# Splitting the gate of a Mamba-2 mixer group in two, and moving its state-space part behind a column tile

## The chip, the cores and the metric

The kernel runs on one core of one Trainium2 chip. The metric is the device time of one execution in microseconds (us); the median of a few runs is given with the lowest and the highest. The engines are called as the profile calls them: PE (matrix products) with its weight loads PEld, DVE (VectorE), ACT (ScalarE), POOL (GpSimd) and SP (SyncE, which issues the DMAs).

## The reference, cut to what matters

The program is one step of a decoder layer for 256 prompt tokens and 8 sample tokens (264 columns): a half-step feed-forward block, a token mixer, a second half-step feed-forward block and a per-layer embedding. The change is in the mixer. One projection gives 81 column tiles of 128 features, and 8 state-space groups share them: a group has one tile each of B and C, three of x and three of z. Cut to the state-space part:

```python
proj = u @ w_in                       # -> glu_a, glu_b, z, xbc, dt_raw
v = glu_a * sigmoid(glu_b)            # 8 tiles; causal convolution of width 31, LayerNorm, swish
xbc = silu(causal_dwconv(xbc, ...))   # width 4 -> xs, B, C
dt = softplus(dt_raw + dt_bias)
y, h_new = ssd(xs, dt, a, B, C, d_skip, h0)   # chunked scan, chunks of 128 tokens
yg = y * silu(z)                      # the gate
yg = yg * rsqrt(mean(yg * yg over the group's 384 features) + EPS) * ssm_norm_g
out = concat([v, yg]) @ w_out
```

## The kernel before, in words

Features lie on partitions and tokens on columns. A column tile of a projection is 48 products on PE: 16 row tiles times 3, because weights and activations are split into two float32r halves (lines 244 to 246). The weights are streamed: a load on SP's queue (L150, two of 512 KB a column tile), a rounding on ACT (`whi`, L151), the remainder on DVE (`wlo`, L152). A result goes to one of five `acc` banks in PSUM; three further banks (`ps`) serve all the smaller products.

The loop over `IN_ORDER` goes through the projection's tiles: first dt, then for each group g the tiles B, C, x0, x1, x2, z0, z1, z2, and in groups 1, 2, 4 and 6 a pair of GLU tiles (gb, ga) behind x0; the last four GLU pairs (4 to 7) follow group 7. What happens to a finished tile:

- B, C, x: `do_conv`, a short convolution (ACT, then DVE) and a SiLU on ACT. The three x tiles of a group share a buffer `xt`, its three z tiles a buffer `zs`. `xt`, `zs` and the result `y` come from one tag, `h`, with four buffers (the trace calls all of them h).
- `decays(g)`, behind x0: loads of cumulated decays, and Exps on ACT.
- `ssd(g, ...)`, the state-space part, behind x2: transposes on PE (L688, L689), products (L702, L714, L729, L736), the first write of `y` (a DVE operation on the products of L729), then the sample tokens: two transposes (L742, L743), a copy, a store to DRAM and a broadcast load (`d_bc`, `cbc`), three loads of saved state with a product on POOL and a sum on DVE each, and a few small DVE operations, the last of which completes `y`.
- `gate(g, y, zs)`: a DVE product y * zs, three squares on ACT, two adds on POOL (`run`), the sum over partitions on PE (`total`, L296), Ln and Exp on ACT, and the scaled results on DVE. It is put into `pend` at z2 and run by `finish_gate` at the next group's x0, behind that tile's convolution and ahead of `decays`. That of group 7 runs behind GLU tile pair 4, and then the mixer's buffers are given up.
- GLU: three Exp/Ln operations on ACT and a product; the 30 steps of its convolution are put into a queue of filler operations (`bg`), of which the loop takes up to four behind each column tile.

What sets the order: the framework lists each engine's instructions when the program is built. It keeps an estimate of the time, and among the instructions whose inputs and buffers are ready by it, the one earlier in the program goes first; weight loads are marked to go ahead. The engines then run through these lists in order and wait for each other by semaphores. One order is written out by hand: functions on ACT that need a table (SiLU, Sigmoid, Exp, Ln) run in program order (`table`, `after`), so that the table changes only where the program changes from one kind to the other.

Of the kernel before, what the change touches and what calls it, by code (L numbers as in the profile page):

```python
# [41 lines left out]
# ---------------------------------------------------------------- layout plan  # L42
def _in_order():
    """Column tiles of the input projection in the order they are computed."""
    out = [("dt", MT_DT)]
    glu = 0

    def pair():
        nonlocal glu
        out.append(("gb", MT_B + glu))  # L50
        out.append(("ga", MT_A + glu))
        glu += 1

    for g in range(GRP):
        out.append(("B", MT_BM + g))
        out.append(("C", MT_CM + g))
        out.append(("x", MT_X + 3 * g))
        if g in GLU_IN:
            pair()
        out.extend(("x", MT_X + 3 * g + j) for j in (1, 2))  # L60
        out.extend(("z", MT_Z + 3 * g + j) for j in range(3))
    while glu < CM:
        pair()
    return out
# [5 lines left out]
def _plan():  # L70
    """Weight units in order of use: (matrix, row tiles, column tiles), row tile slowest."""
# [39 lines left out]
# columns of the small-parameter block  # L111
# [13 lines left out]
class Weights:  # L125
    """Streams the weight units: load, round to float32r, keep what rounding left."""
# [8 lines left out]
    def load(self, between=()):  # L135
        """The next unit, in halves; runs a function of `between` ahead of each half."""
# [29 lines left out]
def kernel(ctx: ExitStack, tc: tile.TileContext, a: dict):  # L166
# [10 lines left out]
    # ------------------------------------------------------------ helpers  # L177
# [50 lines left out]
    def table(name):  # L228
        """Functions that need a table run in program order, so that tables change only here."""
        if order["set"] != name:  # L230
            order["set"] = name
            after(nc.scalar.preload_act_table_set(name).ins)
# [15 lines left out]
    def split(x, gain=None):  # L248
        """float32r halves of x (times a gain per partition)."""
        t = act_tile()  # L250
        if gain is None:
            nc.scalar.copy(t[:, 0, :], x)  # L252
            tt(t[:, 1, :], x, t[:, 0, :].bitcast(F32), ALU.subtract)
        else:
            act(t[:, 0, :], x, AF.Identity, scale=gain)
            stt(t[:, 1, :], x, gain, t[:, 0, :].bitcast(F32), ALU.mult, ALU.subtract)
        return t

    class SumSq:
        """Sum of squares over tiles and partitions, on every partition. The last `direct` tiles  # L260
        go to the tensor engine by themselves."""
# [19 lines left out]
        def add_plain(self, s):  # L281
            """Adds the tile s itself."""
# [16 lines left out]
    def rsqrt(out, x, bias=0.0, scale=1.0):  # L299
        """(scale * x + bias) ** -0.5"""  # L300
        act(out, x, AF.Ln, bias=bias, scale=scale)
        act(out, out, AF.Exp, scale=-0.5)

    def rms_scale(p, n):
        """1 / sqrt(p / n + eps)"""
        r = rtile()
        rsqrt(r, p, eps1, 1.0 / n)
        return r

    # ------------------------------------------------------------ constants  # L310
# [10 lines left out]
    # ------------------------------------------------------------ residual stream  # L321
# [5 lines left out]
    bg = deque()  # work that fills in between the matrix products  # L327

    # ------------------------------------------------------------ feed-forward
# [22 lines left out]
    def ffn(xs, sq, done):  # L352
        """xs: split gained input; sq: its sum of squares. Calls done(m, y) on each finished
        column tile y (without the input scale); returns eps * (mean square + eps) of the input."""
# [42 lines left out]
    def ffn_scale(p, eq):  # L397
        """1 / 2 / sqrt(mean(y^2) + eps / scale^2): the post-norm of scale * y, halved, where
        eq = eps / scale^2."""
# [13 lines left out]
    # ============================================================ FFN 1  # L413
# [15 lines left out]
    # sample conv history: sums over the saved rows  # L429
# [33 lines left out]
    # y for the post-norm; h . y and y . y (with the gain) for the next pre-norm  # L463
# [22 lines left out]
    # mean square of h + rs y, from the parts  # L486
# [8 lines left out]
    # per-layer embedding projection: independent of the residual stream  # L495
# [13 lines left out]
    # u = rmsnorm(h + rs y), two tiles behind the update of h  # L509
# [15 lines left out]
    # ============================================================ mixer  # L525
# [3 lines left out]
    # causal triangle: row token s, column token l, l >= s  # L529
# [6 lines left out]
    tm = mp.tile([P, 2, 2, NH], F32, name="tm")          # token-major dt, dt*A per chunk  # L536
    acs = mp.tile([P, 2, NH], F32, name="acs")           # token-major cumulative sums
    dte = mp.tile([P, 2, NH], F32, name="dte")           # decay to the end of the chunk
    cd = mp.tile([P, NH], F32, name="cd")                # decay over chunk 1
    dtp = mp.tile([P, 24, NS], F32, name="dtp")          # sample dt on (head, p)  # L540
    eap = cpool.tile([P, 24, NS], F32, name="eap")       # sample decay on (head, p)
    xds = cpool.tile([P, 24, NS], F32, name="xds")       # sample x * dt on (head, p)
# [55 lines left out]
    def do_conv(acc, i, out):  # L598
        """Short causal convolution and SiLU of xBC tile i."""
# [9 lines left out]
    def keep(k, x):  # L609
        """A finished input tile of the output projection."""  # L610
# [46 lines left out]
    def decays(g):  # L657
        """Decay between the tokens of each chunk, and from the start of chunk 1."""
# [19 lines left out]
    def ssd(g, bf, cf, xt, ab, ea):  # L678
        """State-space part of group g: y before the gate, [128, 3, T]."""
        hs = slice(HPG * g, HPG * g + HPG)  # L680
        y = h_tile()[:, :3, :]
        # token-major x * dt and B
# [20 lines left out]
        # decay times C.B; the decay's exponent is never positive where l >= s  # L703
# [4 lines left out]
        # state after each chunk  # L708
# [15 lines left out]
        # outputs  # L724
# [14 lines left out]
        # sample tokens  # L739
# [29 lines left out]
    def gate(g, y, zs):  # L769
        tt(y, y, zs, ALU.mult)  # L770
        sq = SumSq(3, direct=0)
        for j in range(3):
            sq.add(y[:, j, :])
        t = tmp()
# [6 lines left out]

    def finish_gate():
        if pend:
            gate(*pend.pop())

    first = gemm_first(us, k16, 4)
    pend = []
    nglu = 0
    for n, (kind, m) in enumerate(IN_ORDER):
# [6 lines left out]
        elif kind == "C":  # L796
            do_conv(acc, m - MT_X, bct[:, 1, :])
        elif kind == "x":
# [7 lines left out]
            if j == 2:  # L806
                y = ssd(g, bct[:, 0, :], bct[:, 1, :], xt, ab, ea)
        elif kind == "z":
# [3 lines left out]
            act(zs[:, j, :], acc, AF.Silu)  # L812
            if j == 2:
                pend.append((g, y, zs))
        elif kind == "gb":
            pb = acc
        elif kind == "ga":
            do_glu(nglu, pb, acc)
            nglu += 1
            if nglu == len(GLU_IN) + 1:  # L820
                finish_gate()
# [9 lines left out]
    # output projection: the state-space rows, then the convolution rows  # L831
# [50 lines left out]
    # ============================================================ FFN 2  # L882
# [3 lines left out]
    def update(j, bb):  # L886
        """Sample state of head pair j: decay and add x dt (outer) B."""
# [37 lines left out]
    # ============================================================ per-layer embedding  # L925
# [32 lines left out]
# tiles (first, count) that each engine brings up to date in the last update  # L958
# [4 lines left out]
# ---------------------------------------------------------------- launch  # L963
# [16 lines left out]
def _feat(v):  # L980
    """(F, ...) -> [128, F/128, ...], feature = tile * 128 + partition."""
# [103 lines left out]
```

## Time and profile before

| | |
|---|---|
| runs | median 2482.04 us of 3 (2472.21 to 2486.53) |
| profiled execution, from its first to its last instruction | 2479.2 us |
| PE busy | 2405.7 us, 97% |
| DVE busy | 1593.6 us, 64% |
| ACT busy | 1179.2 us, 48% |
| POOL busy | 348.6 us, 14% |
| mean granted PE clock | 0.990 |
| DMA | 489.88 MB, mean 198 GB/s |

The profile gives no other time of its own execution than this span; it is 0.1% under the median of the runs. Busy times overlap, and PE's products are pipelined: a row gives a product some 0.28 us, though the next one starts 0.12 us later. "Idle before" or a bracket behind a row is the time that the engine stood still, with the instruction that ended it. The granted clock is the share of PE's full clock that the throttle let through.

### The profile page before, as it was taken

The page shows a single profiled execution, that of the slowest core. Times are in us where ns is not written, and L with a number is a line of the kernel's source. Part 1 is how long each engine was busy: PE and PEld are TensorE (multiplying, and loading weights), DVE is VectorE, ACT ScalarE, POOL GpSimd, SP SyncE. Part 2 cuts the span into 40 slices and gives each one's busy share as a digit, 9 for nine tenths or more (in the row PEclk, how much of TensorE's full clock was granted, in tenths as well). Part 3 has the DMA queues.
Part 4 walks back from the last instruction along what each step waited for, and adds up shares of the span by engine and source line. Part 5 has one row for each costly group of instructions (what it writes and reads, how often), then busy time and mean ns, then how long its engine had stood idle before and what let it go on. Part 6 is the DMA issues. An engine that isn't in the chain of part 4 may idle for free.

```text
span 2479.2 us, 47214 instructions
## 1 busy us (share of the span) xinstructions
PE 2405.7 (97%) x19432; PEld 2380.9 (96%) x19432; DVE 1593.6 (64%) x2249; ACT 1179.2 (48%) x1761; POOL 348.6 (14%) x329
## 2 busy tenths in 40 slices
PE   8999999999999999999999999899999999999996
PEld 8999999999999889999998999899999999999996
DVE  6554455545557858979898965855545655555585
ACT  6444444433456465555655454544444443344463
POOL 2500000000015212121112011410000000000142
PEclk9999999999999999999999999999999999999998
DMA  7655555555556665666665547467666776675653
GB/s 242 211 181 180 180 179 179 180 180 181 181 167 214 200 199 191 214 208 197 210 212 187 180 162 231 140 232 235 221 211 221 237 236 206 210 239 191 193 171 114
DMA packets 160201, 489.88 MB, mean 198 GB/s; under 512 B 23360, under 2 KB 40304, under 8 KB 159984
## 3 DMA queue, kind: packets, MB, share of 16 engines
q1 hardware_dynamic: 159984, 486.85, 60.9%
q8 instruction: 152, 2.49, 0.4%
q14 instruction: 65, 0.53, 0.1%
HBM read 465.65 MB, written 22.42 MB: 197 GB/s over the span
## 4 chain that ended last, share of the span: by engine, by line
PE 86%; DVE 7%; DMA 2%; ACT 2%; issue 2%; POOL 1%; SPq 0%; DVEq 0%; ACTq 0%; POOLq 0%
PE acc L244 28%; PE acc L246 28%; PE acc L245 28%; DVE wlo L152 2%; DVE y L213 1%; DVE h L210 1%; DVE tmp L213 1%; ACT whi L151 1%; DVE act L213 1%; PE ps L729 1%; PE ps L296 0%; POOL run L210 0%; DMA ab<-d_cs 0%; PE ps L714 0%; DMA wraw<-in_w 0%
## 5 line engine op out<-in xcount | busy, mean ns | idle before, releaser
L244 PE MATMUL acc<-act,whi 128*128 128x264 f32 x6320 | 1801.0, 288 | 16.8 <-ACT whi L151 8.4
L245 PE MATMUL acc<-act,whi 128*128 128x264 f32 x6320 | 1804.2, 286 | 12.5 <-DVE act L213 6.3
L246 PE MATMUL acc<-act,wlo 128*128 128x264 f32 x6320 | 1802.4, 286 | 3.6 <-DVE wlo L152 3.6
L152 DVE TENSOR_TENSOR wlo<-wraw,whi 128x1024 fp32r<-128x1024 f32 (+1 forms) x806 | 992.3, 1233 | 612.7 <-ACT whi L151 610.0
L151 ACT CAST whi<-wraw 128x1024 fp32r<-128x1024 f32 (+1 forms) x806 | 828.1, 1031 | 994.7 <-PE acc L245 733.5
L245 PEld LDWEIGHTS acc<-act,whi 128*128 128x128 f32 x6320 | 1203.6, 190 | 17.9 <-DVE act L213 8.6
L246 PEld LDWEIGHTS acc<-act,wlo 128*128 128x128 f32 x6320 | 1199.1, 190 | 7.7 <-DVE wlo L152 5.2
L244 PEld LDWEIGHTS acc<-act,whi 128*128 128x128 f32 x6320 | 1186.6, 189 | 19.9 <-ACT whi L151 8.4
L210 POOL TENSOR_TENSOR run<-run,tmp 128x264 f32<-128x264 f32 x135 | 129.8, 962 | 982.3 <-ACT tmp L237 978.8
L210 POOL TENSOR_TENSOR s<-s,eap 128x1024 f32<-128x1024 f32 x24 | 47.3, 1972 | 608.2 <-DMA s<-in_hst 586.4
L213 DVE SCALAR_TENSOR_TENSOR y<-v,vec,y 128x247 f32<-128x247 f32 (+23 forms) x240 | 124.5, 540 | 1.1
L213 DVE SCALAR_TENSOR_TENSOR s<-bb,xds,s 128x128 f32<-128x128 f32 x192 | 52.6, 347 | 62.9 <-POOL s L210 62.9
L210 POOL TENSOR_TENSOR h<-h,cbc 128x1024 f32<-128x1024 f32 x24 | 65.4, 2738 | 165.3 <-DVE y L213 72.1
L210 DVE TENSOR_TENSOR tmp<-acc,rr 128x264 f32<-128x264 f32 x104 | 44.7, 431 | 64.0 <-PE acc L246 63.9
L252 ACT CAST act<-tmp 128x264 fp32r<-128x264 f32 x120 | 48.6, 409 | 62.3 <-DVE tmp L210 47.5
L210 DVE TENSOR_TENSOR tmp<-tmp,acc 128x264 f32<-128x264 f32 x88 | 37.6, 427 | 45.6 <-PE acc L246 44.8
L210 DVE TENSOR_TENSOR act<-tmp,act 128x264 fp32r<-128x264 f32 x120 | 54.3, 457 | 0.0
L210 DVE TENSOR_TENSOR y<-y,acc 128x264 f32<-128x264 f32 x80 | 34.0, 425 | 26.5 <-PE acc L246 26.5
L237 ACT ACTIVATE tmp<-tmp 128x264 f32<-128x264 f32 x112 | 46.8, 418 | 8.3 <-DVE tmp L210 8.0
L237 ACT ACTIVATE tmp<-y 128x264 f32<-128x264 f32 x67 | 28.1, 426 | 42.3 <-DVE y L210 41.2
L213 DVE SCALAR_TENSOR_TENSOR act<-h,vec,act 128x264 fp32r<-128x264 f32 x48 | 35.2, 756 | 6.4 <-ACT act L237 6.4
L237 ACT ACTIVATE act<-h,vec 128x264 fp32r<-128x264 f32 x48 | 23.8, 512 | 31.3 <-POOL h L210 15.2
(148 smaller groups left out, 800.7 us busy)
## 6 DMA issues: line engine op xcount, KB each, us to landing
wraw<-in_w SPq DMA_DIRECT2D x774, 512.0 KB, 4.7
h<-in_hst SPq DMA_DIRECT2D x24, 512.0 KB, 4.9
s<-in_hst SPq DMA_DIRECT2D x24, 512.0 KB, 6.4
out_nss<-s SPq DMA_DIRECT2D x24, 512.0 KB, 2.8
wraw<-in_w SPq DMA_DIRECT2D x32, 256.0 KB, 3.7
ab<-d_cs SPq DMA_DIRECT2D x16, 384.0 KB, 4.2
cbc<-d_bc SPq DMA_DIRECT2D x8, 512.0 KB, 4.2
bb<-d_bc SPq DMA_DIRECT2D x8, 512.0 KB, 7.4
```

Of the source, the lines that this page charges most:

```text
L151: nc.scalar.copy(hi, raw)
L152: nc.vector.tensor_tensor(out=lo, in0=raw, in1=hi.bitcast(F32), op=ALU.subtract)
L210: return (eng or nc.vector).tensor_tensor(out=out, in0=in0, in1=in1, op=op)
L213: return nc.vector.scalar_tensor_tensor(out=out, in0=in0, scalar=scalar, in1=in1, op0=op0, op1=op1)
L237: i = nc.scalar.activation(out=out, in_=in_, func=func, bias=bias, scale=scale)
L244: nc.tensor.matmul(acc, hi, x[:, 0, :], start=first, stop=False)
L245: nc.tensor.matmul(acc, hi, x[:, 1, :], start=False, stop=False)
L246: nc.tensor.matmul(acc, lo, x[:, 0, :], start=False, stop=last)
L252: nc.scalar.copy(t[:, 0, :], x)
L729: nc.tensor.matmul(pd[64 * q : 64 * q + 64, P * c : P * c + P], xdt[c][:, 2 * j + q, :], ab[c][:, 2 * j + q, :], start=True, stop=True,)
```

## The change

The gate becomes two functions. `gate_begin` holds the product with zs, the squares and the adds; `gate_end` the sum over partitions, the Ln and Exp and the results. The first runs at the next group's C tile, behind its convolution, the second where the whole gate stood, at x0. For the last group the first runs behind GLU pair 4, the second behind pair 5, and with it the end of the mixer's buffers. `ssd` is called behind the group's first z tile and its SiLU, instead of behind x2's convolution; so `zs` is now taken from the tag `h` ahead of `y`. No instruction is added or removed. The comments of the file were taken out as well, which is left out here.

```diff
-    def gate(g, y, zs):
+    def gate_begin(g, y, zs):
         tt(y, y, zs, ALU.mult)
         sq = SumSq(3, direct=0)
         for j in range(3):
             sq.add(y[:, j, :])
+        return g, y, sq
+
+    def gate_end(g, y, sq):
         t = tmp()
         rsqrt(t, sq.total(), eps1, 1.0 / 384)
         for j in range(3):
...
+    def begin_gate():
+        if gated:
+            summed.append(gate_begin(*gated.pop()))
+
     def finish_gate():
-        if pend:
-            gate(*pend.pop())
+        if summed:
+            gate_end(*summed.pop())
...
         elif kind == "C":
             do_conv(acc, m - MT_X, bct[:, 1, :])
+            begin_gate()
...
             if j == 0:
                 finish_gate()
                 ab, ea = decays(g)
-            if j == 2:
-                y = ssd(g, bct[:, 0, :], bct[:, 1, :], xt, ab, ea)
         elif kind == "z":
...
             act(zs[:, j, :], acc, AF.Silu)
+            if j == 0:
+                y = ssd(g, bct[:, 0, :], bct[:, 1, :], xt, ab, ea)
             if j == 2:
-                pend.append((g, y, zs))
+                gated.append((g, y, zs))
...
             if nglu == len(GLU_IN) + 1:
+                begin_gate()
+            if nglu == len(GLU_IN) + 2:
                 finish_gate()
                 nc.sync.dma_start(a["xo"], xo)
                 mctx.close()
```

More of the change, by code (lines that the diff above doesn't have):

```diff
@@ L780, in gate @@
             keep(k, o)
+    def begin_gate():
+        if gated:
+            summed.append(gate_begin(*gated.pop()))
     def finish_gate():
-        if pend:
-            gate(*pend.pop())
+        if summed:
+            gate_end(*summed.pop())
     first = gemm_first(us, k16, 4)
-    pend = []
+    gated, summed = [], []
     nglu = 0
```

## The prediction, made before the changed kernel ran

> **What bounds the kernel now.** I read the page first (busy time, the chain that ended last), then the waits of the matrix engine inside the mixer, then the granted clock in small windows, then the timeline around single gates.
>
> ```profile
> span 2479.2 us, 47214 instructions
> PE 2405.7 (97%) x19432; PEld 2380.9 (96%) x19432; DVE 1593.6 (64%) x2249; ACT 1179.2 (48%) x1761; POOL 348.6 (14%) x329
> PE 86%; DVE 7%; DMA 2%; ACT 2%; issue 2%; POOL 1%; SPq 0%; DVEq 0%; ACTq 0%; POOLq 0%
> ```
>
> PE is busy for 97% of the span and carries 86% of the chain. The change adds and removes no instruction, so it can only move the holes in PE's stream. Its code runs in the input projection, whose 81 column tiles go from 803 to 1374 us. One undisturbed column tile of 48 products takes 5.86 us:
>
> ```profile
> 1036.50:1042.36 5.86, 5.86 (x50) 5.86 (x49) 3.61 (x6) 3.82 (x7) 3.16 (x1) 1.00 0.72 233
> ```
>
> (Columns of such a row: stretch, length, then busy us and count on PE, PEld, DVE, ACT, POOL, the granted clock, DMA share and GB/s.) The waits of PE from 829 to 1376 us (total, times, longest):
>
> ```profile
> PE ps L296 <- POOL run L210: 12.3, 7, 2.8
> PE ps L688 <- ACT h L237: 5.0, 2, 3.4
> PE acc L246 <- DVE wlo L152: 2.5, 5, 1.2
> PE acc L244 <- DVE h L213: 1.4, 1, 1.4
> ```
>
> The first row is the gate: its sum over partitions (L296) waits for GpSimd's second add. The second is the state-space part of group 0, waiting for its x tiles. A stall can cost a second time, in clock:
>
> ```profile
> 877.50:880.90 3.40, 3.40 (x18) 3.40 (x17) 1.43 (x2) 3.35 (x8) 0.00 (x0) 0.50 0.70 192
> 935.50:938.95 3.45, 3.45 (x17) 3.25 (x16) 1.96 (x4) 2.87 (x6) 0.00 (x0) 0.51 0.79 272
> 1068.66:1072.07 3.41, 3.41 (x18) 3.41 (x17) 1.62 (x4) 3.33 (x6) 0.00 (x0) 0.50 0.72 238
> 1362.20:1365.60 3.40, 3.40 (x18) 3.40 (x17) 3.33 (x5) 2.03 (x6) 2.44 (x3) 0.50 0.52 152
> ```
>
> In each of these 3.4 us PE was granted half its clock, so each cost 1.7 us. They stand right behind these stalls (PE's timeline, the idle time in brackets), while the stall of 1.39 us left none:
>
> ```profile
> 876.41 0.44 PE L688 MATMUL ps<-ident,h 128*128 128x128 f32 x2 [3.39 <-ACT h L237]
> 935.13 0.88 PE L296 MATMUL ps<-run,ones 128*128 128x264 f32 x2 [2.80 <-POOL run L210]
> 1067.95 0.71 PE L296 MATMUL ps<-run,ones 128*128 128x264 f32 x2 [1.83 <-POOL run L210]
> 1186.92 0.71 PE L296 MATMUL ps<-run,ones 128*128 128x264 f32 x2 [1.39 <-POOL run L210]
> 1360.97 0.71 PE L296 MATMUL ps<-run,ones 128*128 128x264 f32 x2 [2.48 <-POOL run L210]
> ```
>
> So the gates hold 12.3 + 3 x 1.7 = 17.4 us, and the start of group 0 holds 5.0 + 1.7 = 6.7 us. Nothing else in the mixer that the change touches is that large.
>
> At this place the Trainium skill says otherwise: "TensorE: Matmul & The Clock Gate", Part 1, lets the clock fall to half after about 3.4 us of idleness. The trace differs: 1.83 us were enough at 1067.95. By the page's figure the gates would hold 12.3 us alone, and removing their stalls would give 2469.7.
>
> **Part one: the gate is split.** The question is whether the split gives the sum slack. Each engine's order is fixed when the program is built, by a reckoning of when inputs are ready; program order only breaks ties. Gate 3 (program place: behind tile x4.0) runs like this:
>
> ```profile
> 1116.25 0.98 DVE L210 TENSOR_TENSOR h<-h,h 128x792 f32<-128x792 f32 x1
> 1117.65 0.72 ACT L237 ACTIVATE tmp<-h 128x264 f32<-128x264 f32 x2
> 1118.14 1.66 POOL L210 TENSOR_TENSOR run<-run,tmp 128x264 f32<-128x264 f32 x2 [5.08 <-ACT tmp L237]
> 1119.86 0.71 PE L296 MATMUL ps<-run,ones 128*128 128x264 f32 x2 [0.76 <-POOL run L210]
> 1120.41 0.38 PE L688 MATMUL ps<-ident,h 128*128 128x128 f32 x2
> ```
>
> Product (0.98), squares, two adds (1.66), sum: 3.6 us from 1116.25 to 1119.86 without a pause. The product started 0.22 us after the last piece of y (the sample tokens' part, "h<-ych,sy", at 1116.03):
>
> ```profile
> 1116.03 0.18 DVE L210 TENSOR_TENSOR h<-ych,sy 128x24 f32<-128x24 f32 x1
> 1094.90:1119.84 24.94, 24.20 (x198) 23.99 (x197) 18.07 (x24) 15.74 (x30) 10.12 (x5) 1.00 0.74 240
> ```
>
> x4.0's last product had started at 1094.8 (48 products a tile, counted from the projection's start), and 197 more, four tiles and five products, went by before the sum. Counted in the same way the eight sums come 3.3 to 5.5 tiles behind their place in the program. So what begins the gate is y, not the program place, and one tile of program order is not what PE lacks: the sum is put into PE's stream at the product where it is reckoned ready, and it is late there because the chain on DVE, ACT and POOL takes longer than reckoned. Moving begin one tile ahead and leaving finish where it was leaves both of these as they are. I take 0 us. Gain bound: all stalls gone, -17.4. Loss bound: every gate as bad as the first, 8 x (2.8 + 1.7) = 36 instead of 17.4, +18.6. POOL's own adds show that this can move, since equal adds take 740 to 1794 ns:
>
> ```profile
> L210 POOL TENSOR_TENSOR run<-run,tmp x16: 740/826/1794, 931.6 to 1360.1; 128x264 f32<-128x264 f32 x16
> ```
>
> Instructions that change place here: per group one product, three squares and two adds. No DMA, and no function that needs a table.
>
> **Part two: the state-space part goes behind the first z tile.** All its instructions move: 50 on PE, its DVE, ACT and POOL work, and its six DMAs on SP's queue (d_bc, cbc, three h loads, one state store), now in program behind z0's products, its SiLU and four filler operations. They wait for more than that tile, however. At 1120.41 above, the first two transposes (L688) of the next state-space part follow the gate's sum at once, though x4.0's SiLU was done at 1105; the other six need the SiLUs of x4.1 and x4.2, which are held behind the gate's Ln and Exp by the written table order. By the same count PE is past z0 when those six come, in every group. Only the first pairs of groups 4 and 6 (behind z4.0's fifth product, at z6.0's first) would be sent behind z0, by at most 5.9 us, and nothing uses them before the other six are there. SP's and POOL's queues hold nothing of z0 that these steps would now stand behind but its weight loads, which go first in any case; no wait is added, and what queues behind the gate's wait stays PE's next products and, on ACT, every later Exp and SiLU. 0 us; the bounds are -6.7 (group 0's stall gone) and rival two below.
>
> What really changes is buffers. Three h buffers were free at 1129, yet the z SiLUs, the first of whose tiles was done at 1126 (43 products behind the sum above), came only at 1143, beside the first write of y:
>
> ```profile
> 1129.08 0.74 ACT L237 ACTIVATE h<-h 128x264 f32<-128x264 f32 x2
> 1143.29 0.95 ACT L237 ACTIVATE h<-acc 128x264 f32<-128x264 f32 x3
> 1144.01 0.47 DVE L213 SCALAR_TENSOR_TENSOR h<-h,vec,ps 128x256 f32<-128x256 f32 x1
> ```
>
> It is so in all eight groups: buffers of one tag go out in program order, y first. Now zs comes first, so z0's SiLU can follow x2's, some 14 us sooner, and its acc bank is free as much sooner. What would that buy? PE waited for an acc bank once, 1.4 us (the row "acc L244" above, at 1000.91), and there the banks were held by GLU tiles and late convolutions, not by z. 0 us, bound -1.4. If this cover went, z tiles would hold three of five banks again, as now.
>
> **Part three: the last gate** moves behind the GLU tile pair 5. Its Exp stood in the table order behind gate 7:
>
> ```profile
> 1361.72 0.48 ACT L237 ACTIVATE tmp<-ps,eps 128x264 f32<-128x264 f32 x1 [0.77 <-PE ps L296]
> 1362.72 0.38 ACT L237 ACTIVATE v<-acc 128x264 f32<-128x264 f32 x1
> ```
>
> It goes ahead now, some 20 us sooner, and gives DVE its 30 filler operations sooner. PE did not wait for those; the sum of gate 7 still waits for y. 0 us. The tables change at the same places, so the 18 loads stay:
>
> ```profile
> L232 ACT ACT_TABLE_LOAD x18 | 23.1, 1283 | 0.3
> ```
>
> **Sum:** 0 + 0 + 0. The profiled execution stays at 2479.2; its span is 0.1% under the median of 2482.04, which I forecast again: 2482.
>
> **The rivals.** *One, the split works:* the begin gets ahead, the sums are ready before PE comes, and the stalls with their half-clock stretches vanish: 2482.0 - 17.4 = 2464.6. For it: the stall is exactly the POOL add that the split puts earlier, and the z SiLUs and last GLU tile give ACT and DVE more room. Against it: the product follows y at once in the rows of gate 3.
>
> *Two, slower:* the state-space part of a group starts a tile later, the next gate comes a tile later, and the GLU tiles, whose Exps stand behind the gate in the table order, hold their acc banks a tile longer. At 1000.91, with gate 1 five tiles behind, PE had run out of banks for 1.4 us. One tile more would cost up to 5.9 us in each of the four groups with a GLU pair, and a half-clock stretch each: 4 x (5.9 + 1.7) = 30.4, 2512. It decides from a lag of about six tiles on. Against it: lags shrink from 5.5 tiles at gate 0 to 3.3 at gate 6, and z gives its banks back sooner.
>
> *Three, the same mechanism with other lengths:* the new order puts POOL's adds beside other DVE work, and stalls go toward the loss bound: up to 2482 + 18.6 = 2500.6.
>
> **How the numbers follow.** No real effect: 0.62, with a spread of its own of 9 us either way (half of the 17.4 or 18.6). Rival one 0.18, rival two 0.12, rival three 0.08. A measurement of this kernel tells about 0.5%, 12.4 us, from no change. Rival one counts as faster, and 0.02 of the main case with it: 0.20. Rivals two and three give slower, nearly all of it: 0.18. The rest, 0.62, is same. The range reaches down to rival one, 2465, and up to near the end of rival three, 2498, and leaves rival two and the far ends out.
>
> **What the profile of the changed kernel would show.** Right: PE's wait L296 <- POOL stays at 9 to 16 us in six to eight places; L688 follows L296 at once; z0's SiLU follows x2's within 2 us instead of 14, ahead of y's first write; the Exp of GLU pair 5 stands ahead of the last gate's Ln; 18 table loads; three to five half-clock stretches in the mixer. Wrong: a wait L296 <- POOL under 5 us (rival one), which would mean that the sum is placed by program order after all; waits "acc <- ACT v" or "acc <- DVE h" of some us in groups 1, 2, 4 and 6 (rival two); adds mostly above 1200 ns (rival three).

## The result and the profile after

The changed kernel took 2489.91 us (median; 2488.0 to 2490.01), the kernel before 2479.74 us in the same comparison (a fourth run joined the three that gave 2482.04): a ratio of 1.0043, with a 95% interval of 1.0022 to 1.0064. No change had been forecast; it is 0.4% slower, a little under the 0.5% that I had taken for the limit of a measurement, but the interval leaves out 1.

The page of the changed kernel, its span, its busy times and its shares of the chain that ended last, hardly differs from that of before: the same work, 7.1 us more span. The seven instructions more are ones that handle semaphores; the counts of PE, DVE, ACT and POOL are those of before.

```profile
span 2486.3 us, 47221 instructions
PE 2404.2 (97%) x19432; PEld 2378.8 (96%) x19432; DVE 1594.3 (64%) x2249; ACT 1180.7 (47%) x1761; POOL 354.2 (14%) x329
PE 84%; DVE 7%; issue 3%; ACT 2%; DMA 2%; POOL 1%; SPq 0%; DVEq 0%; POOLq 0%; ACTq 0%
```

The waits of PE from 829 to 1386 us (total, times, longest) look as forecast at first sight, 10.5 us on the gates instead of 12.3. But there are four instead of seven, and one of them is 8.0 us:

```profile
PE ps L296 <- POOL run L210: 10.5, 4, 8.0
PE acc L246 <- DVE wlo L152: 9.2, 7, 2.7
PE ps L688 <- ACT h L237: 3.9, 2, 3.5
PE acc L244 <- DVE sy L210: 3.1, 1, 3.1
PE acc L244 <- ACT v L237: 1.5, 1, 1.5
```

PE's timeline at the sums of gates 0, 2, 3 and 5 and at the other stalls behind 1361 (idle time in brackets, none where PE did not wait) show where they lie. The stalls of gates 0 to 6 add up to 2.5 us, where those of before had 9.8 (12.3 less the 2.48 of the last). The large one is the last gate's, and three waits for the weights' remainders stand ahead of it:

```profile
935.61 0.71 PE L296 MATMUL ps<-run,ones 128*128 128x264 f32 x2 [0.90 <-POOL run L210]
1074.13 0.61 PE L296 MATMUL ps<-run,ones 128*128 128x264 f32 x2
1130.35 0.71 PE L296 MATMUL ps<-run,ones 128*128 128x264 f32 x2 [1.11 <-POOL run L210]
1251.07 0.71 PE L296 MATMUL ps<-run,ones 128*128 128x264 f32 x2 [0.51 <-POOL run L210]
...
1364.75 0.39 PE L246 MATMUL acc<-act,wlo 128*128 128x264 f32 x1 [1.94 <-DVE wlo L152]
1368.46 0.59 PE L246 MATMUL acc<-act,wlo 128*128 128x264 f32 x1 [2.71 <-DVE wlo L152]
1370.44 0.59 PE L246 MATMUL acc<-act,wlo 128*128 128x264 f32 x1 [0.30 <-DVE wlo L152]
1379.69 1.25 PE L296 MATMUL ps<-run,ones 128*128 128x264 f32 x2 [8.00 <-POOL run L210]
1382.41 0.59 PE L244 MATMUL acc<-act,whi 128*128 128x264 f32 x1 [1.48 <-ACT v L237]
```

The windows around that place show the clock (columns as in the prediction; the figure behind POOL's is the granted clock). In the 3.4 us ahead of the fall PE worked for 1.00; then the clock was half for 20.5 us:

```profile
1366.80:1387.30 20.50, 9.07 (x34) 7.71 (x35) 16.61 (x38) 5.89 (x16) 8.81 (x6) 0.50 0.21 64
1387.30:1390.70 3.40, 3.40 (x30) 3.40 (x30) 3.40 (x12) 1.85 (x3) 0.00 (x0) 1.00 0.04 6
1363.40:1366.80 3.40, 1.00 (x6) 0.79 (x6) 3.40 (x9) 0.00 (x0) 0.00 (x0) 1.00 0.60 195
```

All this falls into one column tile. I counted products in the two traces, 48 to a tile, for a ledger of starts:

| | before | after | difference |
|---|---|---|---|
| input projection, first product | 803.4 | 803.0 | -0.4 |
| output projection, first product | 1374.5 | 1361.7 | -12.8 |
| its first 48 products take | 5.8 | 26.0 | +20.2 |
| second feed-forward block, first product | 1568.3 | 1575.5 | +7.2 |

So the input projection became 12.4 us shorter. Most of that is the 7.3 us that gates 0 to 6 wait less, the 2.5 us of the last gate's stall, whose sum now stands in the next projection, and 1.7 us of half clock (5.1 us there instead of 6.8). The first 48 products of the next projection gave 20.2 back: 8.0 + 4.9 + 1.5 of stalls, and most of the rest is half clock: PE worked for 9.07 of the 20.5 us, and half of that is lost. From the 49th product of the output projection to the last one of the kernel both traces take 1078.2 us. The ledger is that of the two profiled executions, 7.1 us apart; the medians lie 10.2 apart.

**Why the last sum is late.** The last piece of y (`h<-ych,sy`) is what the gate waits for. The timelines of DVE, first before and then after, show it for groups 2, 6 and 7:

```profile
1061.38 0.17 DVE L210 TENSOR_TENSOR h<-ych,sy 128x24 f32<-128x24 f32 x1
1302.24 0.17 DVE L210 TENSOR_TENSOR h<-ych,sy 128x24 f32<-128x24 f32 x1
1355.26 0.18 DVE L210 TENSOR_TENSOR h<-ych,sy 128x24 f32<-128x24 f32 x1
```

```profile
1069.78 0.17 DVE L210 TENSOR_TENSOR h<-ych,sy 128x24 f32<-128x24 f32 x1
1310.98 0.17 DVE L210 TENSOR_TENSOR h<-ych,sy 128x24 f32<-128x24 f32 x1
1371.17 0.17 DVE L210 TENSOR_TENSOR h<-ych,sy 128x24 f32<-128x24 f32 x1
```

y is complete 8.4, 8.7 and 15.9 us later, while PE comes to the end of the projection 12.8 us sooner. Over all eight groups the lag is 2.3, 2.9, 8.4, 9.5, 8.3, 9.3, 8.7 and 15.9 us: it is not made anew in each group but handed on, and it grows most from group 1 to group 2 and in the last one. The handing on shows in group 4: its last x SiLUs come 9.1 us later (1138.17 in the rows below, 1129.08 in the prediction's), since the written table order holds them behind gate 3's Ln and Exp, and the sum of gate 3 came 10.5 us later (1130.35 instead of 1119.86). What the last group adds is shown below, with e14. Seven sums have tiles enough behind them, and there a later y costs nothing: the builder puts those sums further back in PE's stream (6.0 to 6.5 tiles behind the place where the gate's begin stood before, 3.3 to 5.5 before). The eighth has only the few tiles that are left.

**What the group does differently.** The timelines of ACT and DVE in the changed kernel, group 4: the z SiLUs (`h<-acc`) follow the x SiLUs (`h<-h`) at once, and y's first write comes 15 us behind them, at 1154.00; before, that write was at 1144.01, beside the z SiLUs (the prediction's rows).

```profile
1138.17 0.74 ACT L237 ACTIVATE h<-h 128x264 f32<-128x264 f32 x2
1138.82 0.93 ACT L237 ACTIVATE h<-acc 128x264 f32<-128x264 f32 x3
...
1153.61 0.47 DVE L213 SCALAR_TENSOR_TENSOR bc<-acc,vec,bc 128x253 f32<-128x253 f32 x1
1154.00 0.86 DVE L213 SCALAR_TENSOR_TENSOR h<-h,vec,ps 128x256 f32<-128x256 f32 x2
```

### The profile page after: what moved, and what is told of

The parts are those of the page before. It is cut to its first block, busy times and chain, and to the rows that moved or that the text cites. A ratio compares the mean times of both kernels' runs of the same rounds, so it can differ in the third digit from the quotient of the medians.

```text
span 2486.3 us, 47221 instructions
## 1 busy us (share of the span) xinstructions
PE 2404.2 (97%) x19432; PEld 2378.8 (96%) x19432; DVE 1594.3 (64%) x2249; ACT 1180.7 (47%) x1761; POOL 354.2 (14%) x329
## 4 chain that ended last, share of the span: by engine, by line
PE 84%; DVE 7%; issue 3%; ACT 2%; DMA 2%; POOL 1%; SPq 0%; DVEq 0%; POOLq 0%; ACTq 0%
PE acc L244 28%; PE acc L246 27%; PE acc L245 27%; DVE wlo L152 2%; DVE y L213 1%; DMA ab<-d_cs 1%; DVE h L210 1%; DVE tmp L213 1%; ACT whi L151 1%; ACT ab L237 1%; DVE act L213 0%; PE ps L296 0%; POOL run L210 0%; PE ps L729 0%; PE ps L714 0%
## 5 line engine op out<-in xcount | busy, mean ns | idle before, releaser
L244 PE MATMUL acc<-act,whi 128*128 128x264 f32 x6320 | 1799.3, 288 | 19.6 <-ACT whi L151 8.2
L246 PE MATMUL acc<-act,wlo 128*128 128x264 f32 x6320 | 1800.3, 286 | 10.5 <-DVE wlo L152 10.3
L245 PEld LDWEIGHTS acc<-act,whi 128*128 128x128 f32 x6320 | 1201.9, 190 | 21.0 <-DVE act L213 10.5
L246 PEld LDWEIGHTS acc<-act,wlo 128*128 128x128 f32 x6320 | 1197.1, 190 | 15.1 <-DVE wlo L152 13.5
L244 PEld LDWEIGHTS acc<-act,whi 128*128 128x128 f32 x6320 | 1186.0, 189 | 23.5 <-ACT whi L151 11.7
L213 DVE SCALAR_TENSOR_TENSOR y<-v,vec,y 128x233 f32<-128x233 f32 (+19 forms) x240 | 121.7, 532 | 1.1
L237 ACT ACTIVATE act<-h,vec 128x264 fp32r<-128x264 f32 x48 | 23.8, 512 | 30.7 <-DVE h L210 15.5
```

Source lines behind the costliest of these rows:

```text
L213: return nc.vector.scalar_tensor_tensor(out=out, in0=in0, scalar=scalar, in1=in1, op0=op0, op1=op1)
L237: i = nc.scalar.activation(out=out, in_=in_, func=func, bias=bias, scale=scale)
L244: nc.tensor.matmul(acc, hi, x[:, 0, :], start=first, stop=False)
L245: nc.tensor.matmul(acc, hi, x[:, 1, :], start=False, stop=False)
L246: nc.tensor.matmul(acc, lo, x[:, 0, :], start=False, stop=last)
```

## The experiments

Each ratio is to the kernel before on the same chip, with its 95% interval. "First output product" is the start of the output projection (1374.5 before, 1361.7 after). A place such as ga7+0 means: in PE's order the sum stands behind that many products of that tile (out: of the output projection). Before, the last two sums stand at z7.1+14 and gb7+2; after, at ga4+9 and out:24.

| run | ssd behind | median | ratio | last sum at | first output product |
|---|---|---|---|---|---|
| e1, split only | x2 | 2480.81 | 1.0004 (0.9993 to 1.0014) | gb7+19 | 1374.4 |
| e2, ssd only | z0 | 2490.04 | 1.0040 (1.0026 to 1.0054) | ga7+0 | 1383.7 |
| e3, old tail | z0 | 2488.81 | 1.0036 (1.0024 to 1.0048) | ga7+0 | 1381.5 |
| e4, zs called for first | x2 | 2479.63 | 1.0002 (0.9988 to 1.0016) | gb7+2 | |
| e7, zs written first | x2 | 2488.16 | 1.0038 (1.0024 to 1.0052) | ga7+0 | 1384.3 |
| e8, y written first | z0 | 2496.75 | 1.0073 (1.0060 to 1.0087) | out:24 | 1378.2 |
| e13, zs in its own buffer | x2 | 2488.06 | 1.0029 (1.0020 to 1.0038) | ga7+0 | 1380.7 |
| e5, late last sum | z0 | 2482.61 | 1.0008 (0.9999 to 1.0018) | out:104 | 1365.3 |
| e6, the same, split only | x2 | 2477.21 | 0.9991 (0.9981 to 1.0002) | out:144 | 1371.0 |
| e9, e5 with half the fillers | z0 | 2478.31 | 0.9987 (0.9977 to 0.9997) | out:104 | 1364.1 |
| e10, before with half the fillers | x2 | 2480.02 | 1.0001 (0.9990 to 1.0011) | gb7+2 | 1373.9 |
| e14, e5 with 7 of 30 fillers | z0 | 2472.14 | 0.9958 (0.9946 to 0.9971) | out:144 | 1362.7 |
| e15, e5 with fillers later | z0 | 2480.42 | 1.0007 (0.9998 to 1.0016) | out:104 | 1365.4 |
| e16, e6 with fillers later | x2 | 2477.82 | 0.9997 (0.9988 to 1.0006) | out:144 | 1374.4 |
| e11, e5 with five pairs in the groups | z0 | 2485.01 | 1.0018 (1.0007 to 1.0029) | out:144 | 1369.6 |
| e12, e6 with five pairs in the groups | x2 | 2475.84 | 0.9983 (0.9973 to 0.9993) | out:144 | 1367.2 |

### Which part of the change does it (e1, e2, e3)

e1 is the changed kernel with `ssd` back at x2; e2 the kernel before with `ssd` moved; e3 the changed kernel with the last gate at its old place.

```diff
 # e1, against the changed kernel; e2 is the reverse move in the kernel before
+            if j == 2:
+                y = ssd(g, bct[:, 0, :], bct[:, 1, :], xt, ab, ea)
...
-            if j == 0:
-                y = ssd(g, bct[:, 0, :], bct[:, 1, :], xt, ab, ea)
 # e3, against the changed kernel
                 begin_gate()
-            if nglu == len(GLU_IN) + 2:
                 finish_gate()
```

> The changed kernel with the state-space part back behind x2; the split gate and the late end of the last gate stay. Theory A (the buffer order zs before y, brought by the moved state-space part, frees the middle of the mixer; the late end of the last gate loses the tail): the middle is that of before, waits L296 <- POOL about 12 us over gates 0 to 6, and the tail loses as in the changed kernel or less, so 2484 to 2494 us, ratio 1.002 to 1.006. Rival B (the split itself frees the middle): waits of gates 0 to 6 under 4 us, the projection ends near 1362 us. Rival C (a later state-space part, not pair 5, puts the last gate into the output projection): no stall of 8 us at the last gate, ratio 0.998 to 1.001.

> The kernel before with only the state-space part moved behind z0; the gate whole, the last one behind pair 4 as before. Theory A: the middle gains about 12 us as in the changed kernel and the tail does not lose, so about 2468 us, ratio 0.994 to 0.997. Rival B (the split frees the middle): waits L296 <- POOL about 12 us as before, ratio 1.000 to 1.004. Rival C (the later state-space part makes the last gate late): a stall of some 5 to 8 us at the last gate, ratio 1.002 or more.

> The changed kernel, but the last gate begins and ends behind GLU pair 4, as before. Theory A: the projection's middle as in the changed kernel, and the last gate stalls PE by less than 3 us, because the 30 filler operations of pair 5 come after it and POOL's add is not starved: 2466 to 2474 us, ratio 0.994 to 0.998. Rival C: the last gate still stalls PE by 5 us or more in the output projection, ratio 1.002 to 1.005.

The split alone is the kernel before; the moved `ssd` alone is the changed kernel. The new place of the last gate makes no difference to the time: without it the last sum stands 72 products sooner (ga7+0 instead of out:24) and stalls longer, with a shorter half-clock stretch (17 us). PE's waits of e1, of e2 and of e3:

```profile
PE ps L296 <- POOL run L210: 12.3, 6, 3.2
```

```profile
PE ps L296 <- POOL run L210: 14.6, 4, 11.8
```

```profile
PE ps L296 <- POOL run L210: 15.2, 4, 11.5
```

In the last two nearly all of the wait is one stall, that of the last gate. Rival C has the ratio of all three runs (its stall of 5 to 8 us is 11.8 in e2), theory A of none: the place behind pair 5 was not to blame.

### What in the moved ssd does it (e4, e7, e8, e13)

The move changes two things: the program place of the state-space part, and who gets a buffer first, zs or y. e4 calls for the buffer of zs ahead of `ssd` in the kernel before; e7 also writes one column of it there, on POOL; e8 does the same for y in the changed kernel; e13 gives zs a tag of its own in the kernel before.

```diff
 # e7, against the kernel before (e4: without the memset)
             if j == 2:
+                zs = h_tile()[:, :3, :]
+                nc.gpsimd.memset(zs[:, 0, :1], 0.0)
                 y = ssd(g, bct[:, 0, :], bct[:, 1, :], xt, ab, ea)
...
-            if j == 0:
-                zs = h_tile()[:, :3, :]
 # e8, against the changed kernel; ssd is given this y
+            if j == 2:
+                y = h_tile()[:, :3, :]
+                nc.gpsimd.memset(y[:, 0, :1], 0.0)
 # e13, against the kernel before
-                zs = h_tile()[:, :3, :]
+                zs = mp.tile([P, 3, T], F32, tag="zs", bufs=1, name=nm("zs"))
```

> The kernel before with one line moved: the buffer zs is taken from the tag h ahead of y, at x2, and nothing else changes place. Theory A (buffer order): the z SiLUs follow x2's SiLU within 2 us, and the middle gains as in the changed kernel, about 12 us: ratio 0.994 to 0.997. Rival D (the place of the state-space part in the priority, not the buffers, does it): z SiLUs earlier but waits L296 <- POOL about 12 us as before, ratio 0.999 to 1.001.

> The kernel before, with zs taken and written (one column set to zero on GpSimd, overwritten later by the SiLU; eight small instructions more) ahead of the state-space part, which stays behind x2. The run with zs taken but not written left the order of the SiLUs as it was, so a buffer is handed out at its first write. Theory A2 (the buffer order alone does what the moved state-space part did): z SiLUs right behind x2's, gates 0 to 6 wait under 4 us, the last gate waits 8 to 12 us at gb7 or ga7, ratio 1.002 to 1.006. Rival D2 (the lower rank of the state-space part does it): sums where they were before, waits about 12 us over all gates, ratio 0.999 to 1.001.

> The changed kernel, with y taken and written (one column set to zero on GpSimd) at x2, so that y stands ahead of zs in the tag as before, while the state-space part stays behind z0. Theory A2: with the old buffer order the z SiLUs wait beside y's first write again, sums and waits are those of the kernel before up to the last gate, whose late end puts its sum into the output projection: 2476 to 2486 us, ratio 0.998 to 1.003. Rival D2: as the changed kernel, ratio 1.003 to 1.006.

> The kernel before, with zs taken from a tag of its own with one buffer, so that the z SiLUs neither wait for y nor stand ahead of it; ssd stays behind x2, ahead of z0. Theory H (what lengthens the chain is that the z SiLUs are let go early, freed from y's first write, not that zs holds the earlier buffer): the eight sums come at the places of the changed kernel (z1.2+1 ... ga4+9, ga7+0), the last one stalls 11 to 12 us, median 1.003 to 1.005 of before, as with the memset on zs. Rival R (y loses time because it gets its buffer behind zs): y has its buffer as early as before here, so the sums come at the old places and the median is 0.999 to 1.001.

e4 did nothing: on PE, DVE, ACT and POOL its order is that of before, instruction for instruction. Calling for a buffer first does not put it first; with e7 beside it, it is the first write that counts. e7 leaves `ssd` at x2 and gives the whole effect: all eight sums at the places of e2, and the last stall (PE's timeline):

```profile
1373.18 1.25 PE L296 MATMUL ps<-run,ones 128*128 128x264 f32 x2 [11.88 <-POOL run L210]
```

e13 gives it too, with y's buffer as early as before:

```profile
1369.86 1.25 PE L296 MATMUL ps<-run,ones 128*128 128x264 f32 x2 [11.72 <-POOL run L210]
```

So neither the program place of `ssd` nor a later buffer for y is needed for the loss; it is enough that the z SiLUs are let go early. In e13 y's first write of group 4 comes at 1154, as after. Counted in products, the state-space part's own products lie further apart in PE's stream then: in group 4, 25 products between the two of L714 and 15 from the second to the last of L729 before, 37 and 30 after and in e13. Why the builder's reckoning spreads them so was not found, and the spread does not explain the lag: from the last x SiLUs to y's first write group 4 took 14.9 us before and 15.8 after, and in group 7 the products lie about as close as before (27 and 15 before, 25 and 18 after). e8, where the z SiLUs come early as well (1140 in group 4), was slower than either theory had it: it stalls in all eight gates, 20.5 us, and has seven half-clock stretches behind 829. What y's earlier buffer costs there stays open. PE's waits of e8:

```profile
PE ps L296 <- POOL run L210: 20.5, 8, 6.7
```

### Is it the last sum (e5, e6)

Both put the end of the last gate, and the splitting of its three result tiles, ahead of the fourth weight unit of the output projection (`gemm_first` calls the function there); e6 with `ssd` at x2.

```diff
             if nglu == len(GLU_IN) + 2:
-                finish_gate()
...
+    def last_gate():
+        finish_gate()
+        for k in range(CM + 21, CM + 24):
+            outk[k] = split(outk[k])
...
-    accs = gemm_first(outk, list(range(CM, CM + 24)), 6)
+    accs = gemm_first(outk, list(range(CM, CM + 24)), 6, last_gate)
```

> The changed kernel with the end of the last gate put still later in the program: ahead of the fourth of the six units of four row tiles that open the output projection, whose last unit alone needs it (the sum then stands 104 products into that projection, not 24). Theory E (the chain through the eight state-space parts ends after PE has run out of products that may go ahead of the last sum; the changed kernel loses by the place of that one sum): the wait of some 8 us and most of the 20 us at half clock behind it go, so 14 to 20 us less than the changed kernel, 2470 to 2476 us, ratio 0.996 to 0.999. Rival F (DVE, full with filler operations, holds the weights back anyway): waits for wlo take the place of the sum's, 2485 us or more, ratio 1.002 or more.

> As the run before, but with the state-space part back behind x2: the split gate, and the last sum 144 products into the output projection. Theory E: only the last gate's wait (1.9 to 2.5 us) and its half-clock stretch (1.7 us) go, waits of gates 0 to 6 stay near 10 us: 2474 to 2478 us, ratio 0.998 to 0.9995. Rival F: no gain or a loss, ratio 1.000 or more.

With the moved `ssd` this is worth some 7 us (2489.9 to 2482.6), half of what theory E asked for and more than rival F allowed; without it 3.6 (e1 to e6). The last sum does not stall any more, and the half-clock stretch there falls from 20.5 to 10.2 us. What stays in e5 is the wait for the remainders:

```profile
PE acc L246 <- DVE wlo L152: 9.9, 7, 2.7
PE ps L296 <- POOL run L210: 3.9, 4, 2.0
```

### What makes the remainders late (e9, e10, e14, e15, e16)

DVE is nearly full at the mixer's end in every version that leaves nothing out (18.1 to 20.0 of the 20 us from 1340 to 1360); besides the remainders it runs the state-space part of group 7 and the steps of the GLU convolutions. e9 and e14 leave out 15 and 23 of each 30 such steps in pairs 4 to 7, on top of e5; e10 is e9's edit in the kernel before. e15 and e16 leave nothing out, but take one step from the queue behind each of the last eight tiles instead of four, on top of e5 and e6.

```diff
 # e9, e10: 16; e14: 8
-        for d in range(1, KW):
+        for d in range(1, KW if i < 4 else 16):
 # e15, e16
-        for _ in range(4):
+        for _ in range(1 if n >= 73 else 4):
```

> The run with the late last sum, with half of the filler operations left out for GLU pairs 4 to 7 (15 instead of 30 steps of the wide convolution each, so its output is not the reference's there). Theory G (the gain of the middle, a projection that ends about 9 us sooner, is eaten because DVE is full from 1340 to 1430 us and brings the weight remainders late): without 60 operations of 0.38 to 0.45 us, some 25 us of DVE work, the waits for wlo behind 1360 us and their half-clock stretch go, and the run comes 8 to 12 us under the late-sum run, 2468 to 2474 us, and at least 4 us under the same cut of the kernel before. Rival H (the chain through the last state-space part alone sets the end): 2480 us or more, no gain over the late-sum run.

> The kernel before with the same filler operations left out, as the control. Theory G: PE waits for nothing that these operations cause there (the last gate's sum stalls 2.5 us by its own chain), so 2476 to 2481 us, ratio 0.998 to 1.0005. Rival H: the same.

> The changed kernel with the last sum put ahead of the fourth weight unit of the output projection, and of the 30 convolution steps of GLU pairs 4 to 7 only 7 kept (with 15 kept it was 2478.3, with all 2482.6). If DVE's filler operations are what makes the weights' remainders late at the mixer's end: waits acc <- DVE wlo fall from 8.2 to under 4 us, no half-clock stretch between 1364 and 1380, output projection's end at 1561 or earlier, median 2473 to 2476. If the state-space part and the gate themselves fill DVE there: waits 6 to 9 us, the half-clock stretch stays, median 2477 to 2480.

> The changed kernel with the last sum put ahead of the fourth weight unit of the output projection, and behind the last eight column tiles (GLU pairs 4 to 7) one filler operation taken from the queue instead of four, so that the rest falls into the output projection. Nothing is left out. Theory H: as with the fillers left out, waits acc <- DVE wlo fall to about 4 us and no half-clock stretch stands between 1360 and 1380; the state-space rows of the output projection end at the same lead; the convolution rows may wait for their LayerNorm. Median 2473 to 2478 (0.997 to 0.999 of before). Rival: the fillers come back as a wait of the convolution rows, median 2480 to 2488.

> The same two edits with ssd behind x2 again (the split alone). Theory H: the gates 0 to 6 keep 9 to 12 us of stalls, the last gives none: 2474 to 2479 (0.997 to 0.9995), level with the run that takes the fifth pair into the groups. Rival as for the other run: 2480 to 2488.

The windows of 1340 to 1360 and 1360 to 1380 of e5 and then of e14 show PE's column, the first behind the length, and DVE's, the third:

```profile
1340.00:1360.00 20.00, 20.00 (x170) 19.78 (x167) 19.90 (x30) 7.66 (x9) 5.69 (x3) 1.00 0.53 166
1360.00:1380.00 20.00, 14.90 (x89) 13.86 (x89) 20.00 (x36) 7.94 (x18) 5.06 (x3) 0.75 0.46 151
```

```profile
1340.00:1360.00 20.00, 20.00 (x166) 20.00 (x165) 15.02 (x20) 8.22 (x12) 8.56 (x3) 1.00 0.56 185
1360.00:1380.00 20.00, 20.00 (x166) 20.00 (x165) 19.25 (x37) 11.04 (x18) 1.95 (x2) 1.00 0.62 188
```

With most of the steps gone, DVE has air ahead of 1360, PE runs through 1360 to 1380 without a pause at full clock, the waits for remainders fall to 4.1 us, and the time is 0.42% under that of before: the shorter input projection is worth something once its end is clear. (The kernel before was run with half the steps only, so how much of the 0.42% is the steps' own is not separated.) Half of the steps gave less than I had expected of them (2478.3 instead of 2468 to 2474), since DVE was still full from 1340 to 1360 (19.94 of 20); and in the kernel before leaving out half bought nothing (e10).

The same steps also lengthen the way of y itself. Group 7, from y's first write to its last piece, with the convolution steps that DVE ran between the two:

| | before | after | e3 | e5 | e14 |
|---|---|---|---|---|---|
| y's first write | 1324.74 | 1335.33 | 1338.13 | 1338.97 | 1336.39 |
| y's last piece | 1355.26 | 1371.17 | 1366.29 | 1374.79 | 1361.73 |
| from one to the other | 30.5 | 35.8 | 28.2 | 35.8 | 25.3 |
| steps between (us of DVE) | 10 (9.1) | 28 (19.5) | 21 (14.7) | 28 (19.5) | 9 (4.3) |

Of the 15.9 us by which y of the last group was late, 10.6 stood at its first write, and 5.3 came on the way behind it. From e5 to e14, whose edits differ by the steps alone, the way falls from 35.8 to 25.3 us.

e15 missed its expectation: put later in the program, the steps still fill DVE from 1340 to 1440, with 9.7 us of waits for the remainders, as in e5. A later place in the queue does not hold them back. The same edit on the split alone (e16) is level with the kernel before (0.9997), and not, as expected, with e12. So no complete kernel keeps e14's gain here.

### A better version (e11, e12)

The queue has less to do at the end if a fifth GLU pair runs inside the groups.

```diff
-GLU_IN = (1, 2, 4, 6)
+GLU_IN = (1, 2, 3, 4, 6)
```

> The late-sum run with one GLU pair more inside the projection (a pair in group 3 too), so that three instead of four pairs follow group 7; nothing is left out. Theory G: 30 filler operations leave the full stretch of DVE and run in group 3, where DVE was busy 38 of 52 us: waits for wlo at the start of the output projection shrink, 2472 to 2478 us, ratio 0.997 to 0.9995. Rival H (the chain is the bound; 11.7 us less of PE's own work is left behind the last state-space part): ratio 1.001 or more.

> As the run before, with the state-space part back behind x2 (the split gate, the late last sum, a pair in group 3 too). Theory G: 2472 to 2478 us, no better than with the state-space part behind z0 by more than 3 us. Rival H: ratio 1.000 or more.

With `ssd` at z0 (e11) a new wait takes the place of the old ones, one of 7.0 us for a bank held by a GLU tile (`acc L244 <- ACT v`), and the run is slower than before, as rival H had it. With `ssd` at x2 (e12) it pays: 2475.84 us, 0.17% faster than before with an interval that leaves out 1, and with the clock at 0.993 in the profiled execution. It beats both kernels and leaves nothing out, and it is 9.2 us ahead of e11 where at most 3 had been expected. The fifth pair alone, in the kernel before, was not run, so what the split and the late sum add to it is not shown. Its waits, from 829 to 1400:

```profile
PE ps L296 <- POOL run L210: 11.0, 6, 2.9
PE ps L690 <- ACT h L237: 4.5, 2, 3.1
PE acc L246 <- DVE wlo L152: 3.3, 5, 1.1
```

## Why the prediction was right and where it was wrong

**The bound and the 17.4 us that the gates hold:** right as a reading of before, and the price of half clock behind a stall, too. The gates' stalls could be had (9.8 to 2.5 us for gates 0 to 6), which I had thought only the split could do.

**Part one, the split, 0 us:** right, and e1 shows it: sums at nearly the same places, the same 12.3 us, ratio 1.0004. What begins the gate is y.

**Part two, 0 us:** this is the step that failed. It had the effect on the buffers right (though it is the first write that counts, not the place in the program): zs takes the earlier one, and z0's SiLU follows x2's within 1 us instead of 14. But it priced that by one thing alone, PE's wait for an acc bank (1.4 us), and took the time of y for unchanged. In the trace y came 8.4 us later by group 2 and 15.9 by group 7, and in e13, where the state-space part stays and the z SiLUs go early, 8.4 and 10.6. The term set at 0, with bounds of -6.7 and rival two's 30, measured -12.4 in the input projection and +20.2 behind it, net +7.2. Both parts were missed for one reason: the sum's place in PE's stream had been seen to come from the builder's reckoning, but I did not ask what a freed engine queue does to that reckoning, nor that the last group has no tiles left to hide a later sum. The row of the last stall before (2.48 us at 1360.97, 13.5 us ahead of the projection's end) was the hint.

**Part three, the last gate, 0 us:** the number is right (e3 against the changed kernel, 2488.8 against 2489.9), by luck. The fillers that the place lets through sooner (pair 5's Exp came 34 us sooner, not 20, at 1329.0) were not free: 28 instead of e3's 21 convolution steps stood in the way of group 7's y, which was complete 4.9 us later, and POOL's first add of that gate ran beside such steps for 4.93 us, where e3 has no add above 1.23. The sum's wait ended 9.4 us later than in e3 (1379.69, not 1370.31); that its place was 72 products later, some 8.8 us of PE's work, hid about as much.

**The rivals.** One named the waits that vanished, for another reason, and without their gain. Two named the lag of six tiles that came (6.0 to 6.5), but not its place or price: one wait for a bank grew, from 1.4 to 3.1 us in group 1, with a half-clock stretch behind it, and none came in groups 2, 4 and 6. Three had the sign and the size (2489.9 lies between 2482 and 2500.6), but its adds above 1200 ns were not there: their median is 834 ns after, 826 before. None had the end of the chain.

**The signs to look for.** The wait "9 to 16 us" came (10.5), but in four places instead of six to eight, most of it in one: a total would have passed where the count and the longest did not. L688 follows L296 at once (1130.90 behind 1130.35), the Exp of pair 5 (1329.0) stands ahead of the last gate's Ln (1381.0), and the table loads are 18, all as forecast. Half-clock stretches were three, within the three to five of the forecast by count, but of 6.8, 3.4 and 20.5 us: the four before had 13.7 us in all, these have 30.7.

**The limit of the measurement:** the comparisons told 0.1 to 0.2% apart, not 0.5%.

## What to carry to other kernels

A stall inside a long stream and a stall at its end have different prices: before shortening the waits of early rounds, ask which round is last, and what is left to run beside it. When a program is ordered by a reckoning, freeing one engine's work moves that of the others; follow the completion time of the value that ends the chain through all rounds, not the waits. Work that only fills gaps is not free where the chain's last value needs the same engine. And compare the count and the longest of a wait, not its sum.

## What the runs showed of the hardware

A half-clock stretch need not follow one long stall. The clock fell at 1366.8, behind a window of 3.4 us in which PE had worked for 1.00, where one pause of 1.94 us had ended and the next had lasted 1.05; and it stayed at half for six such lengths, all but the last of which held a part of a stall. The Trainium skill, "TensorE: Matmul & The Clock Gate", Part 1, puts the fall behind about 3.4 us of idleness; these rows show it with PE idle for 2.4 of 3.4 us.

Equal adds on POOL took 737 to 1822 ns, but the first add of the last gate took 4930 in the changed kernel, beside a run of 14 convolution steps on DVE without a pause (and 4552 in e8, beside such a run too). The timelines of DVE and of POOL, whose row holds both adds of the last gate, and the adds of the mixer in one line (shortest, median, longest in ns):

```profile
1372.91 5.31 DVE L213 SCALAR_TENSOR_TENSOR y<-v,vec,y 128x242 f32<-128x242 f32 x14
```

```profile
1373.89 5.75 POOL L210 TENSOR_TENSOR run<-run,tmp 128x264 f32<-128x264 f32 x2 [14.02 <-ACT tmp L237]
```

```profile
L210 POOL TENSOR_TENSOR run<-run,tmp x16: 740/834/4930, 933.8 to 1378.9; 128x264 f32<-128x264 f32 x16
```

In e3 the first add of the last gate meets such a step the other way round. The add takes 739 ns, and the step that starts beside it 1002 instead of 455 (the timelines of DVE and of POOL):

```profile
1368.16 0.46 DVE L213 SCALAR_TENSOR_TENSOR y<-v,vec,y 128x227 f32<-128x227 f32 x1
1368.65 1.00 DVE L213 SCALAR_TENSOR_TENSOR y<-v,vec,y 128x226 f32<-128x226 f32 x1
```

```profile
1368.66 0.74 POOL L210 TENSOR_TENSOR run<-run,tmp 128x264 f32<-128x264 f32 x1 [9.78 <-ACT tmp L237]
```

The Trainium skill, "SBUF — State Buffer", section "SBUF: two separate sides", says that DVE and GpSimd share a pair of ports as an exclusive lock, held for a whole instruction, also by a DVE instruction with two inputs in SBUF. The rows agree: one of the two keeps its pace and the other is held up. That an add waits for a whole run of such instructions, and not for one, is what they suggest, and no run tested it by itself (e2 has the same stall of the last gate with no add above 1232 ns).
